# Compressing the cached pages with 512 columns in place of 256

## The chip, the cores and the metric

The kernel runs on one core of a Trainium2 chip. The metric is the device time of one execution in microseconds. Before the change it is 2870.46 us, the median of three runs (2867.37 to 2870.47).

## What is computed

The program is one step of a decoder layer: a half-step feed-forward network (SwiGLU), a mixer of RWKV-7 and sparse attention (NSA) in parallel, and a second feed-forward half-step, for 256 prompt tokens and 8 x 4 sampled ones, 288 columns in all. The change concerns the compression of the cached keys and values of the sampled sequences. Of the reference this is:

```python
blocks = kv_all[:, :, :2].reshape(b, n_cmp, CMP_BLOCK, 2, G, hd) + cmp_pe[:, :, None, :]
flat = blocks.transpose(0, 1, 3, 4, 2, 5).reshape(b, n_cmp, 2, G, CMP_BLOCK * hd)
hid = jax.nn.gelu(jnp.einsum('bnkgf,kfc->bnkgc', flat, cmp_w1))
kc = jnp.einsum('bnkgc,kcd->bnkgd', hid, cmp_w2)
```

A block is 32 positions of 128 features. There are 8 sequences with 8 pages of 128 positions, so 64 pages with 4 blocks and 2 heads each, which is 512 columns for the keys (k = 0) and 512 for the values (k = 1). Each column is the product of a 32 x 128 long vector with cmp_w1, which has 256 outputs, then GELU, then a product with cmp_w2.

## The kernel before

Every large product runs in split form: a float32 operand becomes a high part (rounded to the type fp32r) and a low part (the rest), and a product is the sum of three matmuls, high x high, low x high and high x low. Weights come in granules of 512 KB, four tiles of 128 x 256. `granule` (L71 to L82) loads one into `raw` (three slots) from the SP queue (L74), and for each half of it ScalarE casts the high part `whi` (L78) and VectorE subtracts to get the low part `wlo` (L80); each of these has four slots of half a granule. `dense_multi` (L129 to L148) takes a block of 256 outputs: two accumulators, and for each granule 24 matmuls with the weights stationary and 288 columns moving (L145 to L147). After each granule it calls `tick`.

Other work is woven into the dense products through a queue of generators. `tick` adds `K.rate` to a credit and takes a step of the first generator for each whole credit (L101 to L106). During the first feed-forward network, after its first pair of blocks, the queue holds `compress_cache`, with a rate of 0.7 (L1635); 256 ticks are left then. The order on each engine is set at compile time by a scheduler that works from this program order, and each engine takes its instructions in that order.

`compress_cache` goes through k = 0 and 1 and, for each, through two halves s of 32 pages. The pages of a half fill `craw`, a tile with one slot, in 8 steps of 4 pages; `page_loads` (L1026 to L1039) reads the page numbers into SP's registers (L1031) and issues one load of 128 KB for each page (L1039). Then come 32 steps, one for each position l of a block. In each ScalarE writes `cxh` (position embedding added, rounded, L1066), VectorE writes `cxl` (L1067), both 128 x 256 with three slots, and TensorE does six matmuls with 256 columns (L1072 to L1075), three for each half of the outputs, all into one bank `sc`. The weights cmp_w1 come through `granule`, a new one every four steps, 8 for each half. At the end of a half there are the GELU (L1080, L1090), the second product in full precision (L1083, L1098), a copy and a store.

Of the kernel before, what the change touches and what calls it, by code (L numbers as in the profile page):

```python
# [108 lines left out]
def drain(K, left=0):  # L109
    while len(K.queue) > left and step(K):  # L110
        pass
# [780 lines left out]
def pst(K, name):  # L892
    return K.ps.tile([128, 512], F32, name=name, bufs=2 if name == "sc" else 1)
# [133 lines left out]
def page_loads(K, pt, dst, src, p0, hist, lag=6, pool=False):  # L1027
    tc, nc = K.tc, K.nc
    n = dst.shape[1]
    eng, kind = (nc.gpsimd, mybir.EngineType.Pool) if pool else (nc.sync, mybir.EngineType.SP)  # L1030
    ins, vals = nc.values_load_multi_w_load_instructions(pt[0:1, p0:p0 + n], engines=[kind], min_val=0,  # L1031
                                                         max_val=src.shape[0] - 1)
    for q in ins:
        if not pool:
            follow(K, q, K.last_dma)
        if len(hist) >= lag:
            follow(K, q, hist[-lag])
    for i in range(n):
        hist.append(eng.dma_start(dst[:, i], src[bass.ds(vals[i], 1)].rearrange("a p f -> (a p) f")))  # L1039


def compress_cache(K, M, sp):
    tc, nc, a = K.tc, K.nc, K.a
    pt = sp.tile([1, 64], I32, name="pt0")
    follow(K, nc.sync.dma_start(pt, a["page_table"]), K.last_dma)
    ppe = sp.tile([128, 2, 32], F32, name="pe0")
    follow(K, nc.sync.dma_start(ppe, a["cmp_pe"]), K.last_dma)
    cw2 = sp.tile([128, 2, 2, 128], F32, name="cw20")
    follow(K, nc.sync.dma_start(cw2, a["cmp_w2"]), K.last_dma)
    hist = []  # L1050
    v8 = lambda t: t.rearrange("p (a b) -> p a b", b=8)
    for k in range(2):
        for s in range(2):
            raw = sp.tile([128, 32, 256], F32, name="craw", bufs=1)
            for p0 in range(0, 32, 4):
                page_loads(K, pt, raw[:, p0:p0 + 4], a["cache_cmp"][:, k], 32 * s + p0, hist)
                yield
            rv = raw.rearrange("p a (l g b) -> p a l (g b)", l=32, g=2)
            acc = pst(K, "sc")
            for gi in range(8):  # L1060
                for q, hi, lo in granule(K, a["cmp_w1"][k, gi]):
                    l = gi * 4 + q
                    pe = ppe[:, k, l:l + 1]
                    xh = sp.tile([128, 256], F32R, name="cxh", bufs=3)
                    xl = sp.tile([128, 256], F32R, name="cxl", bufs=3)
                    nc.scalar.activation(v8(xh), rv[:, :, l], AF.Identity, bias=pe)  # L1066
                    nc.vector.scalar_tensor_tensor(v8(xl), rv[:, :, l], pe, v8(xh.bitcast(F32)), op0=OP.add,  # L1067
                                                   op1=OP.subtract)
# [9 lines left out]
            hid = sp.tile([128, 2, 256], F32, name="chid", bufs=1)  # L1078
            if k == 0:
                nc.scalar.activation(hid.rearrange("p m c -> p (m c)"), acc, AF.Gelu_apprx_tanh)  # L1080
                pk = pst(K, "tp")[:, :256]
                for m in range(2):
                    nc.tensor.matmul(pk, cw2[:, 0, m], hid[:, m], start=m == 0, stop=m == 1)  # L1083
                kc = sp.tile([128, 256], F32, name="kc", bufs=1)
                nc.vector.tensor_copy(kc, pk)
                nc.gpsimd.dma_start(M.kcd[:, 256 * s:256 * s + 256], kc)
            else:
                for m in range(2):
                    for g in range(2):
                        nc.scalar.activation(  # L1090
                            hid[:, m].rearrange("p (b g a k) -> p b g a k", b=4, g=2, a=8)[:, :, g],
                            acc[:, 256 * m:256 * m + 256].rearrange("p (b a g k) -> p b a g k", b=4, a=8, g=2)[:, :, :, g],
                            AF.Gelu_apprx_tanh)
                for pk4 in range(2):
                    pk = pst(K, "tp")[:, :128]
                    for u in range(4):
                        for m in range(2):
                            nc.tensor.matmul(pk[32 * u:32 * u + 32], hid[:, m, 128 * pk4 + 32 * u:128 * pk4 + 32 * u + 32],  # L1098
                                             cw2[:, 1, m], start=m == 0, stop=m == 1, tile_position=(0, 32 * u))
                    vc = sp.tile([128, 128], F32, name="kc", bufs=1)  # L1100
                    nc.vector.tensor_copy(vc, pk)
                    nc.gpsimd.dma_start(M.vcd[:, 2 * s + pk4], vc)
            yield


def attn_prompt(K, M, pool):
# [506 lines left out]
def body(tc, a, o):  # L1613
    nc = tc.nc
    with ExitStack() as ctx:
        K = setup(tc, ctx, a)
        M = Ctx()
# [28 lines left out]
        with pool("x2") as xp:  # L1646
# [124 lines left out]
```

## Time and profile before

| | |
|---|---|
| median of the runs | 2870.46 us (2867.37 to 2870.47) |
| span of the profiled execution, first to last instruction | 2869.0 us |
| TensorE busy | 2800.4 us, 98% |
| VectorE busy | 1721.0 us, 60% |
| ScalarE busy | 1367.9 us, 48% |
| moved by DMA | 506.49 MB, mean 177 GB/s |
| first and last matmul line of the compression (L1072) | 84.2 and 867.8 us |

The profile gives no other time of the profiled execution than its span; it lies 1.5 us under the median of the runs, which were separate executions. Engine names in the rows: PE is TensorE's matmul, PEld its weight load, DVE VectorE, ACT ScalarE, POOL GpSimd, SPq the queue of SyncE that issues loads. A row of a timeline begins with the start in us and the time that it covers; "x3" means that three instructions are merged, and square brackets hold the idle time of the engine before it and what ended it. Matmul records overlap, since their durations are latencies.

### The profile page before, as it was taken

To read this page: it belongs to the slowest core of one execution; us is meant where nothing else is said; L and a number is where in the kernel's file an instruction comes from. 1 tells how busy PE (TensorE), PEld (TensorE's weight loads), DVE (VectorE), ACT (ScalarE), POOL (GpSimd) and SP (SyncE) were. 2 spreads that over 40 slices of the span, in tenths; PEclk is the share of its full clock that TensorE was granted. 3 is DMA by queue.
4 is the path that set the end of the run, shared out by engine and by line. 5 is a ranking of instruction groups with operands and counts; after the bars stand their busy time and mean duration, and the time that the engine had idled before them with its cause. 6 is when DMAs were issued, how large, how long until landed. Compare 5 with 4: busy or idle time off the path is not lost.

```text
span 2869.0 us, 57650 instructions
## 1 busy us (share of the span) xinstructions
PE 2800.4 (98%) x22257; PEld 2691.6 (94%) x22257; DVE 1721.0 (60%) x2950; ACT 1367.9 (48%) x2607; POOL 498.9 (17%) x686
## 2 busy tenths in 40 slices
PE   8999999999999899999999999998999999999997
PEld 8999999999999788998988978998999999999997
DVE  5565565655665777793585765655655455555555
ACT  5555555544555564532344644445444444434443
POOL 2000000000001456521133214112100000000002
PEclk9999999999999999998999999998999999999998
DMA  7557556557555443465446558563556555555553
GB/s 241 175 167 225 169 169 223 171 167 224 168 164 170 161 131 114 130 217 165 119 144 209 167 190 304 184 220 116 176 177 205 165 181 179 188 165 167 165 166 122
DMA packets 171751, 506.49 MB, mean 177 GB/s; under 512 B 28380, under 2 KB 55540, under 8 KB 171220
## 3 DMA queue, kind: packets, MB, share of 16 engines
q1 hardware_dynamic: 158516, 457.65, 50.4%
q0 software_dynamic: 12528, 44.27, 4.8%
q8 instruction: 174, 2.85, 0.4%
q14 instruction: 101, 0.83, 0.1%
q10 hardware_dynamic: 432, 0.88, 0.1%
HBM read 487.39 MB, written 23.66 MB: 178 GB/s over the span
## 4 chain that ended last, share of the span: by engine, by line
PE 93%; DVE 3%; DMA 1%; issue 1%; ACT 1%; POOL 0%; SPq 0%; DVEq 0%; POOLq 0%; ACTq 0%
PE acc L147 27%; PE acc L146 27%; PE acc L145 27%; PE sc L1075 1%; PE sc L1074 1%; PE sc L1072 1%; PE pv L1391 1%; DVE x L246 1%; DMA raw<-in_w_in_dram 1%; PE sc L656 1%; PE sc L1280 1%; DVE f L243 1%; DVE wlo L80 0%; DVE xlo L159 0%; PE sc L661 0%
## 5 line engine op out<-in xcount | busy, mean ns | idle before, releaser
L80 DVE TENSOR_TENSOR wlo<-raw,whi 128x512 fp32r<-128x512 f32 x1568 | 1111.5, 712 | 926.6 <-ACT whi L78 903.9
L78 ACT CAST whi<-raw 128x512 fp32r<-128x512 f32 x1568 | 964.2, 618 | 1202.4 <-PE acc L146 1077.4
L146 PE MATMUL acc<-xlo,whi 128*128 128x288 f32 x4208 | 1256.5, 299 | 12.1 <-DVE xlo L159 12.1
L145 PE MATMUL acc<-xhi,whi 128*128 128x288 f32 x4208 | 1251.3, 299 | 15.1 <-ACT whi L78 11.9
L147 PE MATMUL acc<-xhi,wlo 128*128 128x288 f32 x4208 | 1244.7, 300 | 10.3 <-DVE wlo L80 10.2
L145 PEld LDWEIGHTS acc<-xhi,whi 128*128 128x128 f32 x4208 | 797.7, 190 | 28.0 <-ACT whi L78 12.8
L146 PEld LDWEIGHTS acc<-xlo,whi 128*128 128x128 f32 x4208 | 798.3, 190 | 25.2 <-DVE xlo L159 13.7
L147 PEld LDWEIGHTS acc<-xhi,wlo 128*128 128x128 f32 x4208 | 792.1, 190 | 25.9 <-DVE wlo L80 13.0
L146 PE MATMUL acc<-hlo,whi 128*128 128x288 f32 x1408 | 416.1, 296 | 0.0
L145 PE MATMUL acc<-hhi,whi 128*128 128x288 f32 x1408 | 414.5, 295 | 0.0
L147 PE MATMUL acc<-hhi,wlo 128*128 128x288 f32 x1408 | 413.5, 296 | 0.0
L313 POOL TENSOR_TENSOR ut<-ut,rstd 128x288 f32<-128x288 f32 x88 | 79.7, 925 | 1364.6 <-ACT ut L312 1364.5
L145 PEld LDWEIGHTS acc<-hhi,whi 128*128 128x128 f32 x1408 | 265.0, 188 | 0.2 <-issue 0.2
L146 PEld LDWEIGHTS acc<-hlo,whi 128*128 128x128 f32 x1408 | 264.4, 188 | 0.2 <-issue 0.2
L147 PEld LDWEIGHTS acc<-hhi,wlo 128*128 128x128 f32 x1408 | 263.3, 188 | 0.0
L184 POOL TENSOR_TENSOR ssacc<-ssacc,sq 128x288 f32<-128x288 f32 x78 | 74.9, 960 | 240.3 <-ACT sq L180 237.5
L1067 DVE SCALAR_TENSOR_TENSOR cxl<-craw,pe,cxh 128x256 fp32r<-128x256 f32 x128 | 63.7, 502 | 47.9 <-ACT cxh L1066 41.4
L1066 ACT ACTIVATE cxh<-craw,pe 128x256 fp32r<-128x256 f32 x128 | 64.0, 506 | 53.8 <-PE sc L1075 44.1
L145 PE MATMUL acc<-ghi,whi 128*128 128x288 f32 x256 | 75.5, 295 | 0.0
L147 PE MATMUL acc<-ghi,wlo 128*128 128x288 f32 x256 | 75.3, 295 | 0.0
L146 PE MATMUL acc<-glo,whi 128*128 128x288 f32 x256 | 75.2, 294 | 0.0
L1075 PE MATMUL sc<-cxh,wlo 128*128 128x256 f32 x256 | 72.0, 281 | 0.0
(430 smaller groups left out, 2484.3 us busy)
## 6 DMA issues: line engine op xcount, KB each, us to landing
raw<-in_f_w_dram SPq DMA_DIRECT2D x528, 512.0 KB, 3.5
raw<-in_w_in_dram SPq DMA_DIRECT2D x156, 512.0 KB, 3.6
craw<-in_cache_cmp_dram SPq DMA_DIRECT2D x128, 128.0 KB, 3.8
raw<-in_cmp_w_dram SPq DMA_DIRECT2D x32, 512.0 KB, 4.4
raw<-in_w_out_dram SPq DMA_DIRECT2D x32, 512.0 KB, 3.6
craw<-in_cmp_w_dram POOLq DMA_DIRECT2D x16, 512.0 KB, 4.8
raw<-in_w_br_rw_dram SPq DMA_DIRECT2D x16, 512.0 KB, 5.3
vsel<-in_cache_sel_dram POOLq DMA_DIRECT2D x64, 128.0 KB, 3.9
```

The lines of the kernel that those rows point to most:

```text
L78: nc.scalar.copy(hi, r)
L80: nc.vector.tensor_sub(lo, r, hi.bitcast(F32))
L145: nc.tensor.matmul(ac[m], hi[:, ms], xhi[:, kt], start=first, stop=False)
L146: nc.tensor.matmul(ac[m], hi[:, ms], xlo[:, kt], start=False, stop=False)
L147: nc.tensor.matmul(ac[m], lo[:, ms], xhi[:, kt], start=False, stop=last)
L184: nc.gpsimd.tensor_tensor(self.acc, self.acc, sq, op=OP.add)
L243: return eng.tensor_tensor(u[:, s], u[:, s], r[:, None, :].to_broadcast([128, s.stop - s.start, NT]), op=OP.mult)
L246: return eng.tensor_tensor(x[:, s], x[:, s], u[:, s], op=OP.add)
L313: nc.gpsimd.tensor_tensor(t, t, rstd, op=OP.mult)
L1066: nc.scalar.activation(v8(xh), rv[:, :, l], AF.Identity, bias=pe)
L1067: nc.vector.scalar_tensor_tensor(v8(xl), rv[:, :, l], pe, v8(xh.bitcast(F32)), op0=OP.add, op1=OP.subtract)
L1075: nc.tensor.matmul(ac, lo[:, ms], xh, start=False, stop=l == 31, skip_group_check=True)
```

## The change

The two halves of the pages are no longer two halves of the columns but two halves of the positions: `half` 0 loads positions 0 to 15 of the blocks of all 64 pages, `half` 1 positions 16 to 31. A matmul then has 512 columns, and its two output halves get a bank each, both slots of `sc`. The weights of a position pass once for each k, so `granule` is called 16 times for cmp_w1 and no longer 32 times. A page load now takes half a page's rows: 64 KB, 128 rows of 512 bytes; there are 64 for each half, in 8 steps of 8. The number of steps falls from 160 to 96, and the rate is set to 0.42.

```diff
     for k in range(2):
-        for s in range(2):
-            raw = sp.tile([128, 32, 256], F32, name="craw", bufs=1)
-            for p0 in range(0, 32, 4):
-                page_loads(K, pt, raw[:, p0:p0 + 4], a["cache_cmp"][:, k], 32 * s + p0, hist)
+        accs = [pst(K, "sc") for _ in range(2)]
+        for half in range(2):
+            raw = sp.tile([128, 64, 128], F32, name="craw", bufs=1)
+            src = a["cache_cmp"][:, k, :, 128 * half:128 * half + 128]
+            for p0 in range(0, 64, 8):
+                page_loads(K, pt, raw[:, p0:p0 + 8], src, p0, hist)
                 yield
-            acc = pst(K, "sc")
-            for gi in range(8):
+            for gi in range(4 * half, 4 * half + 4):
                 for q, hi, lo in granule(K, a["cmp_w1"][k, gi]):
...
-                    xh = sp.tile([128, 256], F32R, name="cxh", bufs=3)
-                    xl = sp.tile([128, 256], F32R, name="cxl", bufs=3)
+                    xh = sp.tile([128, 512], F32R, name="cxh", bufs=3)
+                    xl = sp.tile([128, 512], F32R, name="cxl", bufs=3)
...
-                        ac = acc[:, 256 * m:256 * m + 256]
-                        nc.tensor.matmul(ac, hi[:, ms], xh, start=l == 0 and m == 0, stop=False,
-                                         skip_group_check=True)
-                        nc.tensor.matmul(ac, hi[:, ms], xl, start=False, stop=False, skip_group_check=True)
-                        nc.tensor.matmul(ac, lo[:, ms], xh, start=False, stop=l == 31, skip_group_check=True)
+                        nc.tensor.matmul(accs[m], hi[:, ms], xh, start=l == 0, stop=False)
+                        nc.tensor.matmul(accs[m], hi[:, ms], xl, start=False, stop=False)
+                        nc.tensor.matmul(accs[m], lo[:, ms], xh, start=False, stop=l == 31)
...
-            K.rate = 0.7
+            K.rate = 0.42
```

The GELU, the second product, the copy and the store are done once for each k on 512 columns, no longer once for each of two halves on 256.

Three places in the order of instructions, before and after. The first is TensorE at the first step of the compression (`sc` is the accumulator, `cxh` and `cxl` the pieces of activations, `whi` and `wlo` the weights, `acc` the dense product). Before:

```order
L1072 MATMUL sc_1311<-cxh_1318,whi_1314 128x256
L145 MATMUL acc_1276<-xhi_73,whi_1330 128x288
L1074 MATMUL sc_1311<-cxl_1319,whi_1314 128x256
L146 MATMUL acc_1276<-xlo_74,whi_1330 128x288
L147 MATMUL acc_1275<-xhi_73,wlo_1332 128x288
L1075 MATMUL sc_1311<-cxh_1318,wlo_1316 128x256
```

And with the change:

```order
L1072 MATMUL sc_612<-cxh_1965,whi_1961 128x512
L145 MATMUL acc_1890<-xhi_73,whi_1977 128x288
L1073 MATMUL sc_612<-cxl_1966,whi_1961 128x512
L146 MATMUL acc_1890<-xlo_74,whi_1977 128x288
L147 MATMUL acc_1889<-xhi_73,wlo_1979 128x288
L1074 MATMUL sc_612<-cxh_1965,wlo_1963 128x512
```

The pattern is the same with half the matmuls at twice the columns; the other three of the step go into sc_613.

The second place is the SP queue at the end of the page loads of the second filling of `craw`, from the weight load after which the last pages come (`raw` from in_f1_w2 is a weight of the feed-forward network, in_cmp_w1 the compression's own; ISA rows are register instructions). Before:

```order
L74 DMA raw_4000<-in_f1_w2_dram 128x1024
L1039 ISA
L1039 DMA craw_3394<-in_cache_cmp_dram 128x256
L1031 TENSOR_LOAD pt0_572
L1031 ISA x8
L1039 ISA
L1039 DMA craw_3394<-in_cache_cmp_dram 128x256
L74 DMA raw_4075<-in_f1_w2_dram 128x1024
```

Three more pages follow, and then the weight loads go on. With the change:

```order
L74 DMA raw_4788<-in_f1_w2_dram 128x1024
L1031 ISA x10
L1039 ISA
L1039 DMA craw_3541<-in_cache_cmp_dram 128x128
L1039 ISA
L1039 DMA craw_3541<-in_cache_cmp_dram 128x128
L1039 ISA
L1039 DMA craw_3541<-in_cache_cmp_dram 128x128
L74 DMA raw_4822<-in_f1_w2_dram 128x1024
```

Five more pages follow here: eight pages lie behind the weight load raw_4788, where five lay behind raw_4000. At the first filling eight pages and 12 register instructions lie there, at the third eight and 8, each in place of five pages, a register load and 8 register instructions; at the fourth eight pages, a register load and 16 register instructions, in place of seven pages, a register load and 8.

The third place is ScalarE at the start of the same half, where the first activations of the new `craw` are written. Before:

```order
L78 CAST whi_3923<-raw_3921 128x512
L78 CAST whi_3939<-raw_3921 128x512
L78 CAST whi_4002<-raw_4000 128x512
L1066 ACTIVATE cxh_4150<-craw_3394,pe0_574 128x256
L1066 ACTIVATE cxh_4194<-craw_3394,pe0_574 128x256
L1066 ACTIVATE cxh_4246<-craw_3394,pe0_574 128x256
L78 CAST whi_4018<-raw_4000 128x512
```

And with the change:

```order
L78 CAST whi_4675<-raw_4673 128x512
L78 CAST whi_4691<-raw_4673 128x512
L78 CAST whi_4790<-raw_4788 128x512
L1067 ACTIVATE cxh_4862<-craw_3541,pe0_608 128x512
L1067 ACTIVATE cxh_4944<-craw_3541,pe0_608 128x512
L1067 ACTIVATE cxh_5060<-craw_3541,pe0_608 128x512
L338 COPY f_481<-acc_4450 128x288
```

In both, three pieces of activations stand between the two casts of one granule's halves; the second cast, whi_4806 from raw_4788, comes behind the copy. VectorE has its three pieces in the same place, between the two subtractions. At the first and third fillings it is the same; at the fourth both halves of the granule are cast ahead of the three pieces with the change, and one half before.

## Rows read from the trace of the kernel before

**Rows 1.** The page: busy us, share of the span and instructions of each engine.

```profile
PE 2800.4 (98%) x22257; PEld 2691.6 (94%) x22257; DVE 1721.0 (60%) x2950; ACT 1367.9 (48%) x2607; POOL 498.9 (17%) x686
```

**Rows 2.** Busy time by windows (us), with counts, granted clock, DMA share, GB/s.

```profile
36.00:100.00 64.00, 64.00 (x487) 64.00 (x486) 36.82 (x65) 33.05 (x61) 5.59 (x6) 1.00 0.74 227
...
900.00:940.00 40.00, 40.00 (x302) 40.00 (x301) 20.91 (x33) 21.66 (x43) 7.88 (x10) 1.00 0.53 163
```

**Rows 3.** Timeline of TensorE, dense and compression matmuls.

```profile
86.00 0.29 PE L145 MATMUL acc<-xhi,whi 128*128 128x288 f32 x1
...
89.59 0.28 PE L1072 MATMUL sc<-cxh,whi 128*128 128x256 f32 x1
...
95.69 0.28 PE L1072 MATMUL sc<-cxh,whi 128*128 128x256 f32 x1
...
96.04 0.30 PE L145 MATMUL acc<-xhi,whi 128*128 128x288 f32 x1
```

**Rows 4.** Timeline of TensorE, the second product of the compression.

```profile
254.46 1.02 PE L1083 MATMUL tp<-chid,cw 128*128 128x256 f32 x4
```

**Rows 5.** Groups of instructions from 36 to 860 us: busy us, mean ns.

```profile
L80 DVE TENSOR_TENSOR wlo<-raw,whi 128x512 fp32r<-128x512 f32 x521 | 364.1, 702 | 290.3 <-ACT whi L78 284.0 <-PE sc L194 0.9
L78 ACT CAST whi<-raw 128x512 fp32r<-128x512 f32 x520 | 320.6, 620 | 340.3 <-PE acc L146 279.0 <-DMA raw<-in_f_w_dram 28.3 <-PE sc L1074 22.6
...
L1066 ACT ACTIVATE cxh<-craw,pe 128x256 fp32r<-128x256 f32 x128 | 64.0, 506 | 53.8 <-PE sc L1075 44.1 <-DMA craw<-in_cache_cmp_dram 4.4 <-DMA raw<-in_f_w_dram 2.7
L1067 DVE SCALAR_TENSOR_TENSOR cxl<-craw,pe,cxh 128x256 fp32r<-128x256 f32 x128 | 63.7, 502 | 47.9 <-ACT cxh L1066 41.4 <-DMA raw<-in_f_w_dram 4.0 <-DMA raw<-in_cmp_w_dram 2.5
```

**Rows 6.** Timeline of the SP queue in the second page phase.

```profile
270.54 1.37 SPq L1039 DMA_DIRECT2D craw<-in_cache_cmp_dram  x3
272.01 0.38 SPq L74 DMA_DIRECT2D raw<-in_f_w_dram  x1
272.58 2.24 SPq L1039 DMA_DIRECT2D craw<-in_cache_cmp_dram  x2
...
275.55 1.96 SPq L1039 DMA_DIRECT2D craw<-in_cache_cmp_dram  x3
```

**Rows 7.** Timeline of ScalarE at the start of the second half.

```profile
276.85 0.62 ACT L78 CAST whi<-raw 128x512 fp32r<-128x512 f32 x1 [0.98 <-PE acc L146]
278.45 0.62 ACT L78 CAST whi<-raw 128x512 fp32r<-128x512 f32 x1 [0.98 <-PE acc L146]
281.13 1.31 ACT L1066 ACTIVATE cxh<-craw,pe 128x256 fp32r<-128x256 f32 x3 [2.06 <-DMA craw<-in_cache_cmp_dram]
282.35 1.13 ACT L78 CAST whi<-raw 128x512 fp32r<-128x512 f32 x2
```

**Rows 8.** Timeline of VectorE at the same place.

```profile
281.67 1.28 DVE L1067 SCALAR_TENSOR_TENSOR cxl<-craw,pe,cxh 128x256 fp32r<-128x256 f32 x3 [1.88 <-DMA raw<-in_f_w_dram]
282.99 1.29 DVE L80 TENSOR_TENSOR wlo<-raw,whi 128x512 fp32r<-128x512 f32 x2
```

**Rows 9.** ScalarE's last cast ahead of the first, third and fourth half.

```profile
73.06 0.62 ACT L78 CAST whi<-raw 128x512 fp32r<-128x512 f32 x1 [0.96 <-PE acc L146]
...
484.27 0.62 ACT L78 CAST whi<-raw 128x512 fp32r<-128x512 f32 x1 [1.07 <-PE acc L147]
...
690.43 0.62 ACT L78 CAST whi<-raw 128x512 fp32r<-128x512 f32 x1 [0.98 <-PE acc L146]
```

**Rows 10.** VectorE's first subtraction behind the pieces of the same three halves.

```profile
78.20 2.53 DVE L80 TENSOR_TENSOR wlo<-raw,whi 128x512 fp32r<-128x512 f32 x4
...
489.74 0.68 DVE L80 TENSOR_TENSOR wlo<-raw,whi 128x512 fp32r<-128x512 f32 x1
...
695.22 1.90 DVE L80 TENSOR_TENSOR wlo<-raw,whi 128x512 fp32r<-128x512 f32 x3
```

**Rows 11.** DMA issues: KB each, median us from issue to landing.

```profile
kcd<-kc POOLq DMA_DIRECT2D x2, 128.0 KB, 3.8
vcd<-kc POOLq DMA_DIRECT2D x4, 64.0 KB, 3.2
```

More of the change, by code (lines that the diff above doesn't have):

```diff
@@ L1052, in compress_cache @@
     for k in range(2):
-        for s in range(2):
-            raw = sp.tile([128, 32, 256], F32, name="craw", bufs=1)
-            for p0 in range(0, 32, 4):
-                page_loads(K, pt, raw[:, p0:p0 + 4], a["cache_cmp"][:, k], 32 * s + p0, hist)
+        accs = [pst(K, "sc") for _ in range(2)]
[4 more added lines that the diff above has]
+                page_loads(K, pt, raw[:, p0:p0 + 8], src, p0, hist)
                 yield
-            rv = raw.rearrange("p a (l g b) -> p a l (g b)", l=32, g=2)
-            acc = pst(K, "sc")
-            for gi in range(8):
+            rv = raw.rearrange("p a (l b) -> p a l b", b=8)
+            for gi in range(4 * half, 4 * half + 4):
                 for q, hi, lo in granule(K, a["cmp_w1"][k, gi]):
@@ L1063, in compress_cache @@
                     pe = ppe[:, k, l:l + 1]
-                    xh = sp.tile([128, 256], F32R, name="cxh", bufs=3)
-                    xl = sp.tile([128, 256], F32R, name="cxl", bufs=3)
-                    nc.scalar.activation(v8(xh), rv[:, :, l], AF.Identity, bias=pe)
-                    nc.vector.scalar_tensor_tensor(v8(xl), rv[:, :, l], pe, v8(xh.bitcast(F32)), op0=OP.add,
+                    xh = sp.tile([128, 512], F32R, name="cxh", bufs=3)
+                    xl = sp.tile([128, 512], F32R, name="cxl", bufs=3)
+                    nc.scalar.activation(v8(xh), rv[:, :, l % 16], AF.Identity, bias=pe)
+                    nc.vector.scalar_tensor_tensor(v8(xl), rv[:, :, l % 16], pe, v8(xh.bitcast(F32)), op0=OP.add,
                                                    op1=OP.subtract)
@@ L1076, in compress_cache @@
+                        nc.tensor.matmul(accs[m], hi[:, ms], xl, start=False, stop=False)
+                        nc.tensor.matmul(accs[m], lo[:, ms], xh, start=False, stop=l == 31)
                     if l < 31:
                         yield
[L1078 to L1102, printed above, removed]
@@ L1103, in compress_cache @@
-            yield
+        hid = sp.tile([128, 2, 512], F32, name="chid", bufs=1)
+        if k == 0:
+            for m in range(2):
+                nc.scalar.activation(hid[:, m], accs[m], AF.Gelu_apprx_tanh)
+            pk = pst(K, "tp")
+            for m in range(2):
+                nc.tensor.matmul(pk, cw2[:, 0, m], hid[:, m], start=m == 0, stop=m == 1)
+            kc = sp.tile([128, 512], F32, name="kc", bufs=1)
+            nc.vector.tensor_copy(kc, pk)
+            nc.gpsimd.dma_start(M.kcd, kc)
+        else:
+            for m in range(2):
+                for g in range(2):
+                    nc.scalar.activation(hid[:, m].rearrange("p (b g a k) -> p b g a k", b=8, g=2, a=8)[:, :, g],
+                                         accs[m].rearrange("p (b a g k) -> p b a g k", b=8, a=8, g=2)[:, :, :, g],
+                                         AF.Gelu_apprx_tanh)
+            vc = sp.tile([128, 512], F32, name="kc", bufs=1)
+            pk = pst(K, "tp")
+            for b in range(4):
+                for u in range(4):
+                    for m in range(2):
+                        nc.tensor.matmul(pk[32 * u:32 * u + 32, 128 * b:128 * b + 128],
+                                         hid[:, m, 128 * b + 32 * u:128 * b + 32 * u + 32], cw2[:, 1, m],
+                                         start=m == 0, stop=m == 1, tile_position=(0, 32 * u))
+            nc.vector.tensor_copy(vc, pk)
+            nc.gpsimd.dma_start(M.vcd, vc.rearrange("p (b f) -> p b f", b=4))
@@ L1106, in attn_prompt @@
+        yield
 def attn_prompt(K, M, pool):
```

## The prediction

> **What bounds the kernel now.** I read the page first: TensorE is busy 98% of the span, VectorE 60% and ScalarE 48% [rows 1]. A share over the whole run says little, so next I cut out the stretch in which the changed work runs. From 36 us, when the first pages are asked for, to 860 us TensorE has no idle time in any window, and the clock is 1.00; the first of these windows stands in [rows 2], with a later one without any compression. So in this stretch time is worth only what it is worth on TensorE: either a matmul gets cheaper there, or something else gets so late that TensorE has to wait.
>
> Then the spacing of matmuls, start to start, in the timeline. Between 86.00 and 89.59 us, 27 matmuls with 288 columns start: 3.59/27 = 0.133 us each; the window from 900 to 940 us gives 40/302 = 0.1325 [rows 2, 3]. Three with 256 columns, one behind the other, take 95.69 to 96.04: 0.117 us each [rows 3]. I use 132.8 and 118 ns. The durations on the page (some 300 ns) are latencies and overlap; they are no cost.
>
> **The change, part by part.**
>
> *TensorE.* 768 matmuls with 256 columns become 384 with 512. The columns stay 196,608; what may go is a cost per matmul. The trace has no matmul of this form with 512 columns, so I bound it. A line through the two spacings has a slope of (132.8 - 118)/32 = 0.46 ns a column and no constant left over: 118 + 256 x 0.46 = 236 ns, gain 384 x (2 x 118 - 236) = 0. Lower end: four matmuls of the second layer, in full precision with 256 columns, take 1.02 us with 0.378 us for the last one: (1.02 - 0.378)/3 = 0.214 us each, 512 cycles at 2.4 GHz and no surplus [rows 4]. If 512 columns here run as densely, the gain is 384 x (236 - 214) = 8.4 us. I see no reason for a loss. The two spacings of the same form are nearer to the question than a row of another form; with their reading errors I take 234 ns, **a gain of 0.8 us**. The Trainium skill (TensorE: Matmul & The Clock Gate, section Back-to-back issue gap) gives a warm gap of columns/2.4 plus 2.5 ns, which would be 109 ns for 256 columns and 216 for 512. The rows do not agree at 256, so I do not use it; it stands among the rivals by its mechanism, a cost per matmul that long streams hide.
>
> *Splits of weights.* 32 granules become 16: 32 casts of 618 to 620 ns on ScalarE and 32 subtractions of 702 to 712 on VectorE go [rows 5], 20 and 23 us, and 8 MB of loads. The pieces of activations halve in number, 128 to 64 each, at double width: between 1x and 2x the 0.506 and 0.502 us of one [rows 5]. All of it is work beside a TensorE that never waits: **worth nothing**, as long as TensorE stays covered. The second-layer matmuls keep their columns; fewer copies and stores are off the path. The steps go from 160 to 96 and the rate from 0.7 to 0.42, so both queues last 229 of the 256 ticks.
>
> *Page loads on SP.* 128 become 256, at half the bytes and with rows of 512 bytes. One page costs SP (1.37 - 0.33)/2 = 0.52 us; the register part of a step of four costs 2.24 - 0.33 - 0.52 = 1.39 us [rows 6]. A step is thus 3.5 us, at 0.7 steps a tick; with eight pages 8 x 0.52 + about 2.4 = 6.6 us, at 0.42. With one weight load of about 0.4 us [rows 6], SP needs 2.8 us of a tick before and 3.2 after. A tick without compression matmuls is 24 x 0.1328 = 3.19 us. **SP goes from nine tenths of TensorE's pace to all of it** in the four page phases. Behind a page load on SP stand the weight loads.
>
> *The start of each half.* Here I expect the cost. ScalarE takes its work in order. At 281.13 us it begins the first three pieces of activations, after 2.06 us of waiting for the last page; the next weights' cast stands behind them and starts at 282.35 [rows 7]. VectorE does its three pieces from 281.67 and the subtraction for these weights, 0.69 us, only from 282.99 to 283.68 [rows 8]. When does TensorE want it? A half granule is used up every 1.60 us (276.85 to 278.45), and the cast of 278.45, released by TensorE, took the slot just freed, the fourth. The next slot was free at 280.05, so its weights are wanted at 280.05 + 3 x 1.60 = 284.85, the low part two matmuls later, at 285.1. **1.4 us are to spare.** The same sum at the other three starts [rows 9, 10], the low part being due 1.60 + 4.80 + 0.27 = 6.67 us after the last cast: due 79.73, done 78.89, spare 0.8; due 490.94, done 490.42, spare 0.5; due 697.10, done 695.91, spare 1.2.
>
> After the change three things move there. First, the order of SP: between the weight load whose half is cast last and the last page there were 5 pages, 8 register instructions with their load, and a weight load; now 8 pages, 12, 10 and 8 register instructions and a weight load at the first three starts. With 0.52 a page and an estimate of 0.13 per register instruction that is 1.7, 1.5 and 1.2 us later. At the fourth it is 1.5 later, but both halves are cast ahead, worth 1.6. Second, a load of 64 KB lands sooner than one of 128: 3.2 against 3.8 us for stores of this stage [rows 11], so 0.6 back. Third, three pieces of 512 columns: VectorE spaces three of 256 by (1.28 - 0.50)/2 = 0.4 us, so I take 0.8 for 512 (the lower end is a plain subtraction at that width, 0.7 [rows 5]); with the first ScalarE piece longer by 0.3 to 0.4 this is 1.5 us more. TensorE then waits 1.7 - 0.6 + 1.5 - 0.8 = 1.8, 1.5 - 0.6 + 1.5 - 1.4 = 1.0, 1.2 - 0.6 + 1.5 - 0.5 = 1.6 and 0 us: **4.4 us in all**. Lower end: 0, if ScalarE is further ahead there than now. Upper end: without the 0.6 back it is 6.2 us, and a lagging SP adds to that.
>
> **Sum.** The profiled span is 2869.0 us, 1.5 under the median of the runs, 2870.5, and within their spread. 2869.0 - 0.8 + 4.4 = 2872.6; carried to the median, **2874.1 us**, slower by 0.13%. About 0.2% (5.7 us) is what a measurement of this kernel tells from no change. Behind this stretch the instruction order of the mixer shifts by a few rows; I put nothing on it, and 2 us either way into the range.
>
> **The rivals.**
>
> *Everything stays covered.* The casts saved let ScalarE and VectorE run further ahead, and the spare times suffice. Only the 0.8 us remain: 2869.7. For it: TensorE does not wait once now, and fewer bytes move per tick. Against: the slots for split weights are four as before, so nobody can run further ahead than now.
>
> *A cost per matmul goes away.* TensorE gets 384 x 20 to 22 us nearer the lower end: minus 4 (about 225 ns per matmul, a constant of 11 to 12 ns over 2.4 GHz each) to minus 8.4. With the waits covered 2862.1 to 2866.5; with them 2866.5 to 2871. For it: the full-precision rows run without a surplus. Against: the surplus over 2.4 GHz is larger at 288 columns (12.8 ns) than at 256 (11.3), as a rate would have it.
>
> *SP becomes the supply.* If page loads take SP more than the 0.52 us, weights come slower than TensorE uses them, all through a page phase of some 60 us. It decides from about 0.05 us more per page: 64 x 0.05 = 3.2 us a phase is what whole prefetch slots can carry. Three pages took 1.96 in place of 1.37 us once in the trace [rows 6]; at that rate in each group of six pages a phase loses 6 us, of which some 3 are carried; with the 4.4 that is 2870.5 - 0.8 + 4.4 + 4 x 1.5 to 4 x 3, 2880 to 2886.
>
> **How the numbers follow.** My forecast, waits of 2 to 7 us, 0.48: 2871.7 to 2876.7. Everything covered 0.26; a cost per matmul gone 0.14; SP the supply 0.12. The range leaves out most of the last and the end of the third: 2864.5 to 2880. Slower by over 0.2% (above 2876.2): nearly all of SP's 0.12 and about a fifth of the forecast's 0.48, 0.21. Faster by over 0.2% (below 2864.7): half of the third and little else, 0.08. Within: 0.71.
>
> **What would show it.** Right: compression matmuls 0.23 to 0.24 us apart; idle time of TensorE of 1 to 2 us shortly behind the last page of a half, with the low weights on VectorE as releaser, and ScalarE held there for 3 us by a page load. Wrong: spacing of 0.214 to 0.225; no wait of TensorE before 860 us; or waits spread all over the page phases with weight loads late on SP.

## The result, and the profile after

The changed kernel takes **2890.89 us** (median of 4 runs, 2887.52 to 2893.74) against 2870.47 for the kernel before (4 runs, 2867.37 to 2871.09): a ratio of 1.0069 with a 95% interval of 1.0057 to 1.0081. That is slower by 20 us, beyond the upper end of the range, 2880. The profiled execution has a span of 2887.9 us, 18.9 more than before.

The page first: busy TensorE, the clock by slices, and the chain.

```profile
PE 2806.4 (97%) x21869; PEld 2676.1 (93%) x21869; DVE 1686.3 (58%) x2850; ACT 1327.9 (46%) x2503; POOL 493.7 (17%) x682
...
PEclk9999999999999899998999999998999999999998
...
PE 89%; DVE 4%; SPq 2%; DMA 2%; issue 1%; ACT 1%; POOL 0%; ACTq 0%; DVEq 0%
```

Against [rows 1], VectorE and ScalarE have less work, as the change says. What is new is SyncE's queue in the chain of work that ended last, with 2%. The windows of the changed kernel say where it went (columns as in [rows 2]: length, then busy us and instructions of TensorE, its weight loads, VectorE, ScalarE and GpSimd, granted clock, DMA share, GB/s).

```profile
36.00:860.00 824.00, 813.10 (x5802) 793.56 (x5802) 431.65 (x684) 374.59 (x650) 39.43 (x43) 0.99 0.55 175
109.00:119.00 10.00, 7.88 (x46) 7.12 (x44) 6.28 (x10) 5.61 (x11) 1.86 (x2) 0.83 0.41 146
318.00:328.00 10.00, 6.66 (x32) 6.43 (x31) 5.30 (x8) 5.54 (x11) 0.00 (x0) 0.66 0.47 154
529.00:535.00 6.00, 2.90 (x20) 2.43 (x19) 3.54 (x6) 4.02 (x7) 0.00 (x0) 1.00 0.29 103
739.00:747.00 8.00, 5.66 (x29) 5.19 (x29) 6.55 (x12) 5.43 (x10) 0.00 (x0) 0.80 0.57 194
```

Between 36 and 860 us TensorE had no idle time before; now it has 824.00 - 813.10 = 10.9 us, and it lies in the four short windows, one for each half, shortly behind its last page. In three of the four the clock falls as well. Here is the second of them, in TensorE's timeline.

```profile
318.30 0.29 PE L147 MATMUL acc<-hhi,wlo 128*128 128x288 f32 x1
321.93 0.61 PE L145 MATMUL acc<-hhi,whi 128*128 128x288 f32 x1 [3.34 <-ACT whi L78]
322.33 0.44 PE L146 MATMUL acc<-hlo,whi 128*128 128x288 f32 x1
...
327.13 0.38 PE L145 MATMUL acc<-hhi,whi 128*128 128x288 f32 x1
327.35 0.30 PE L146 MATMUL acc<-hlo,whi 128*128 128x288 f32 x1
```

TensorE waits 3.34 us for a cast on ScalarE. Then its matmuls start 0.24 us apart, 1.2 GHz for 288 columns, up to 327.13, where they go back to 0.13. So one wait costs twice: the idle time, and 2.2 us of slow clock. SyncE's queue ahead of that wait:

```profile
307.31 2.17 SPq L74 DMA_DIRECT2D raw<-in_f_w_dram  x2
310.94 1.41 SPq L1039 DMA_DIRECT2D craw<-in_cache_cmp_dram  x3
312.45 1.25 SPq L74 DMA_DIRECT2D raw<-in_f_w_dram  x1
313.90 2.81 SPq L1039 DMA_DIRECT2D craw<-in_cache_cmp_dram  x5
```

ScalarE's timeline:

```profile
311.24 1.14 ACT L78 CAST whi<-raw 128x512 fp32r<-128x512 f32 x2 [2.91 <-DMA raw<-in_f_w_dram]
315.45 0.62 ACT L78 CAST whi<-raw 128x512 fp32r<-128x512 f32 x1 [3.07 <-PE acc L147]
319.13 1.94 ACT L1067 ACTIVATE cxh<-craw,pe 128x512 fp32r<-128x512 f32 x3 [3.06 <-DMA craw<-in_cache_cmp_dram]
...
321.26 0.61 ACT L78 CAST whi<-raw 128x512 fp32r<-128x512 f32 x1
```

And VectorE's:

```profile
319.89 2.08 DVE L1068 SCALAR_TENSOR_TENSOR cxl<-craw,pe,cxh 128x512 fp32r<-128x512 f32 x3 [3.08 <-ACT cxh L1067]
321.91 2.71 DVE L80 TENSOR_TENSOR wlo<-raw,whi 128x512 fp32r<-128x512 f32 x4
```

ScalarE stands 3.06 us before the page that SyncE asked for last, then does three pieces in 1.94 us; the cast that TensorE needs stands behind them and starts at 321.26. In the kernel before, the wait at this start was 2.06 us and TensorE did not notice [rows 7]. The difference shows ahead of it: at 311.24 ScalarE had just waited 2.91 us for weights, and at 315.45 again 3.07. The profile puts this second wait down to a matmul, but the weights that are cast there were asked for at 309.15 and landed at 315.36 by the trace, and TensorE ran out of weights 3 us behind this cast: it too was a wait for weights, and not for TensorE to free a slot. Over 36 to 960 us, ScalarE's waits for transfers in the changed kernel (us in total, times, longest):

```profile
ACT whi L78 <- DMA raw<-in_f_w_dram: 92.0, 57, 3.6
ACT cxh L1067 <- DMA craw<-in_cache_cmp_dram: 16.4, 4, 5.2
```

Before, these were 28.3 us in 18 waits and 4.4 us in 2 [rows 5]. So weights come late off SyncE's queue, mostly in the page phases: some 52 of the 92 us lie there, in 30% of the stretch. Its timeline in the first of them:

```profile
77.57 0.95 SPq L1039 DMA_DIRECT2D craw<-in_cache_cmp_dram  x2
...
79.19 2.92 SPq L1039 DMA_DIRECT2D craw<-in_cache_cmp_dram  x6
82.20 1.65 SPq L74 DMA_DIRECT2D raw<-in_f_w_dram  x2
85.83 0.87 SPq L1039 DMA_DIRECT2D craw<-in_cache_cmp_dram  x2
...
94.02 4.84 SPq L1039 DMA_DIRECT2D craw<-in_cache_cmp_dram  x8
...
102.59 0.87 SPq L1039 DMA_DIRECT2D craw<-in_cache_cmp_dram  x2
```

From one step of eight pages to the next it takes 8.26, 8.19 and 8.57 us. TensorE gives a step 3.19/0.42 = 7.6 us. Over the four whole phases, from first to last page, SyncE takes 62.0, 65.1, 66.1 and 67.9 us and issues 75 weight loads in them: 3.48 us for each, where TensorE uses one in 3.19. In the kernel before it was 136.3 us for 42, 3.25 each.

The register part of a step can be read by itself. These are the register instructions of the page numbers between 44 and 110 us (duration in ns: shortest, median, longest):

```profile
L1031 SPq FUSED_REGOPS  x58: 147/147/159, 44.0 to 102.2; - x58
L1031 SPq TENSOR_LOAD <-pt x7: 525/529/542, 50.1 to 99.4; - x7
```

Start to start, a load takes 0.58 us and each of the eight reads behind it, a FUSED_REGOPS and a short check, 0.255 us: 2.6 us for a step.

The matmuls themselves did what was forecast: the compression matmuls shown occupy 0.24 and 0.23 us to the next start, where one of 256 columns took 0.117 [rows 3].

```profile
331.08 0.40 PE L1073 MATMUL sc<-cxl,whi 128*128 128x512 f32 x1
331.32 0.29 PE L146 MATMUL acc<-hlo,whi 128*128 128x288 f32 x1
331.45 0.40 PE L1074 MATMUL sc<-cxh,wlo 128*128 128x512 f32 x1
331.68 0.29 PE L147 MATMUL acc<-hhi,wlo 128*128 128x288 f32 x1
```

For a balance I added up, for every matmul until the first feed-forward layer ends, the time to the next start, by kind (us). Two of the experiments below stand beside the two kernels; some 1.3 us of other matmuls are the same in all.

| | before | after | pages on GpSimd | the same, four PSUM tiles |
|---|---|---|---|---|
| first matmul starts | 8.0 | 9.6 | 7.5 | 8.3 |
| feed-forward, 288 columns, 6336 | 851.6 | 871.6 | 854.4 | 852.5 |
| compression, 256 or 512 columns | 91.1 | 89.3 | 89.3 | 89.3 |
| second layer of the keys | 1.4 | 0.9 | 0.9 | 0.9 |
| second layer of the values | 2.4 | 4.8 | 4.8 | 2.7 |
| last matmul of the layer starts | 955.6 | 977.3 | 958.0 | 954.8 |

The layer ends 21.7 us later. 20.0 of it lie in the feed-forward matmuls: most of it waits and slow clock, and 1.8 beside the second layer of the values, whose last records stand singly between them (the last experiment shows these rows); 2.4 lie in that second layer itself; 1.5 in a later first matmul, which varies by as much between the other profiled executions; the wide matmuls and the keys give back 1.8 and 0.4. Of 21.7, 2.8 do not reach the end of the program; the time behind this layer differs by a few us from one profiled execution to the next.

"TensorE's excess" in the expectations is a sum of the same kind: the starts between 36 and 960 us, each less the usual spacing of its columns (133, 118 and 233 ns). It was 1.7 us before and 20.7 after. Where a single surplus is above 0.15 us I count it as a wait, else as slow clock: at the four starts that makes 3.0 + 3.8 + 3.4 + 2.7 = **12.8 us of waits** (more than the 10.9 us idle of the window, where a matmul's latency of 0.3 us counts as busy) **and 1.4 + 2.2 + 0.2 + 1.7 = 5.5 us of slow clock**.

### The profile page after: what moved, and what is told of

It reads as the page before. It is cut to its first block, busy times and chain, and to the rows that moved or that the text cites. A ratio compares the mean times of both kernels' runs of the same rounds, so it can differ in the third digit from the quotient of the medians.

```text
span 2887.9 us, 57227 instructions
## 1 busy us (share of the span) xinstructions
PE 2806.4 (97%) x21869; PEld 2676.1 (93%) x21869; DVE 1686.3 (58%) x2850; ACT 1327.9 (46%) x2503; POOL 493.7 (17%) x682
## 4 chain that ended last, share of the span: by engine, by line
PE 89%; DVE 4%; SPq 2%; DMA 2%; issue 1%; ACT 1%; POOL 0%; ACTq 0%; DVEq 0%
PE acc L147 26%; PE acc L145 26%; PE acc L146 26%; SPq L1039 1%; PE sc L1073 1%; PE sc L1074 1%; PE sc L1072 1%; PE pv L1391 1%; DVE wlo L80 1%; DVE x L246 1%; DMA raw<-in_f_w_dram 1%; SPq L1031 1%; DMA raw<-in_w_in_dram 1%; PE sc L656 1%; DVE xlo L159 1%
## 5 line engine op out<-in xcount | busy, mean ns | idle before, releaser
L80 DVE TENSOR_TENSOR wlo<-raw,whi 128x512 fp32r<-128x512 f32 (+1 forms) x1536 | 1093.9, 716 | 964.1 <-ACT whi L78 926.6
L78 ACT CAST whi<-raw 128x512 fp32r<-128x512 f32 (+1 forms) x1536 | 943.0, 618 | 1255.7 <-PE acc L146 1062.8
L146 PEld LDWEIGHTS acc<-xlo,whi 128*128 128x128 f32 x4208 | 798.9, 190 | 27.0 <-DVE xlo L159 13.5
L1068 DVE SCALAR_TENSOR_TENSOR cxl<-craw,pe,cxh 128x512 fp32r<-128x512 f32 x64 | 48.1, 762 | 63.0 <-ACT cxh L1067 59.0
L1067 ACT ACTIVATE cxh<-craw,pe 128x512 fp32r<-128x512 f32 x64 | 45.4, 720 | 60.9 <-PE sc L1074 44.4
L1073 PE MATMUL sc<-cxl,whi 128*128 128x512 f32 x128 | 50.6, 395 | 0.0
```

The costliest lines, as they stand in the source:

```text
L78: nc.scalar.copy(hi, r)
L80: nc.vector.tensor_sub(lo, r, hi.bitcast(F32))
L146: nc.tensor.matmul(ac[m], hi[:, ms], xlo[:, kt], start=False, stop=False)
L1067: nc.scalar.activation(v8(xh), rv[:, :, l % 16], AF.Identity, bias=pe)
L1068: nc.vector.scalar_tensor_tensor(v8(xl), rv[:, :, l % 16], pe, v8(xh.bitcast(F32)), op0=OP.add, op1=OP.subtract)
L1073: nc.tensor.matmul(accs[m], hi[:, ms], xl, start=False, stop=False)
```

## The experiments

Five of the kernels below (fixed page numbers, the kernel before with the changed kernel's page traffic, the two empty steps, the two rates) were executed once, in the profiled execution; for them the span stands, and the excess says more than the span, since spans of the kernel before lay between 2863 and 2874 us beside them. The others have 8 to 11 runs, and ratios are to runs of the kernel before beside them.

The theory after the result: SyncE needs more time to issue a step's pages than TensorE gives it, so weights and pages come late, ScalarE has nothing in hand when it comes to the last page of a half, and waits there in its order. The rivals: the in-order wait and the wider pieces do it whatever SyncE does; or the short rows of 512 bytes are slow to land.

**Pages at fixed numbers, one transfer a step.** This kernel leaves out the lookup of the page numbers.

```diff
-                page_loads(K, pt, raw[:, p0:p0 + 8], src, p0, hist)
+                hist.append(nc.sync.dma_start(raw[:, p0:p0 + 8], src[p0:p0 + 8].rearrange("a p f -> p a f")))
+                follow(K, hist[-1], K.last_dma)
```

> The changed kernel, but the eight pages of a step are loaded by one transfer at fixed page numbers: the same bytes in the same rows of 512, 32 issues on SyncE in place of 256, and no register instruction for them. It leaves out the lookup of the page table. If SyncE's time for issuing pages is what makes the last page and the weights late, TensorE's excess between 36 and 960 us (20.7 us in the changed kernel, waits and slow clock together) falls below 3, and the span is 2865 to 2871. If short rows or the memory traffic make the pages late, or the wider pieces hold ScalarE and VectorE, the excess stays at 10 or more and the span at 2878 or more.

Measured: span 2869.3 us, excess 2.3. The window of this kernel, columns as above:

```profile
36.00:860.00 824.00, 824.00 (x5913) 806.12 (x5913) 445.96 (x701) 382.59 (x664) 39.95 (x43) 1.00 0.57 178
```

TensorE does not wait once, with the same bytes in the same short rows and the same wide pieces. The rows and the pieces alone cost nothing; the 256 issues with their register instructions do (which of the two was not separated). Late landing is not the reason either: in the page phases a weight load landed 4.0 us (median) after its issue in the changed kernel, 4.9 in the kernel before and 4.0 in the kernel with pages on GpSimd below, which does not wait.

**Four pages to a step.**

```diff
-            for p0 in range(0, 64, 8):
-                page_loads(K, pt, raw[:, p0:p0 + 8], src, p0, hist)
+            for p0 in range(0, 64, 4):
+                page_loads(K, pt, raw[:, p0:p0 + 4], src, p0, hist)
...
-            K.rate = 0.42
+            K.rate = 0.56
```

> The changed kernel with four pages to a step, so 16 page steps in a half, and a rate of 0.56 in place of 0.42, so that the queue lasts as many ticks. Pages, issues and bytes are the same, but a tick of a page phase holds 0.56 x (1.39 + 4 x 0.52) + 0.4 = 2.3 us of SyncE's time in place of 3.2. If SyncE's lag in the page phases is the cause, its queue is no longer behind when the last page is asked for; then only the forecast's in-order wait with the wider pieces is left, 0 to 4.4 us: 2868 to 2875. If the in-order wait is enough by itself for the whole cost, whatever SyncE has behind it, the time stays at 2885 to 2893.

Measured: 2870.12 us, ratio to the kernel before 1.0002 (0.9992 to 1.0011). TensorE is busy for all of 36 to 860 us. ScalarE's waits of this kernel over 36 to 960 us:

```profile
ACT whi L78 <- DMA raw<-in_f_w_dram: 17.9, 11, 2.3
ACT cxh L1067 <- DMA craw<-in_cache_cmp_dram: 5.3, 4, 2.0
```

All 256 issues are still there, over a longer time, and the cost is gone. ScalarE still stands up to 2.0 us before a last page with three wide pieces behind it, and that does not reach TensorE: without SyncE's lag the forecast's own 4.4 us are 0.

**The kernel before, with the changed kernel's page traffic.**

```diff
-            for p0 in range(0, 32, 4):
-                page_loads(K, pt, raw[:, p0:p0 + 4], a["cache_cmp"][:, k], 32 * s + p0, hist)
+            for p0 in range(0, 32, 2):
+                page_loads(K, pt, raw[:, p0:p0 + 2], a["cache_cmp"][:, k], 32 * s + p0, hist, halves=True)
...
+            for h in (0, 128):
+                hist.append(eng.dma_start(dst[:, i, h:h + 128],
+                                          src[:, :, h:h + 128][bass.ds(vals[i], 1)].rearrange("a p f -> (a p) f")))
...
-            K.rate = 0.7
+            K.rate = 0.84
```

> The kernel before, with 256 columns moving and its weights split twice, but each page is loaded as two transfers with rows of 512 bytes, two pages to a step, and the rate is 0.84 so that a page phase lasts 19 ticks as in the changed kernel: 256 issues at the changed kernel's pace, 3.1 us of SyncE in a tick of 3.19. If the number of issues on SyncE is the cause, TensorE waits at the four starts as in the changed kernel, and the span grows by 8 to 20 us, to 2877 to 2889. If the three wider pieces behind the last page are the cause, the excess of TensorE stays within 3 us and the span at 2868 to 2873.

Measured: span 2877.9 us, 8.9 more than before, excess 12.7. Its waits, ScalarE's over 36 to 960 us and TensorE's over 36 to 860:

```profile
ACT cxh L1071 <- DMA craw<-in_cache_cmp_dram: 13.8, 4, 4.8
PE acc L145 <- ACT whi L78: 4.6, 4, 2.2
PE acc L147 <- DVE wlo L80: 1.2, 3, 0.8
```

The narrow matmuls with the weights split twice become slow in the same way, at three of the four starts: the page loads do it without the rest of the change. It is the lower end of what was expected, about half the cost of the changed kernel by the span and somewhat more by the excess (11.0 of 19.0 us above the kernel before); whether the other half is due to the wider pieces on top of a late SyncE or to the steps being smaller was not separated.

**Two empty steps behind the last page.**

```diff
+            for _ in range(2):
+                yield
             rv = raw.rearrange("p a (l b) -> p a l b", b=8)
```

> The changed kernel with two empty steps between the last page of a half and its first piece of activations: 104 steps at the same rate of 0.42, some 4.8 ticks or 15 us in which ScalarE and VectorE meet no page. SyncE's page phases are as dense as before. If the cost comes only where ScalarE waits in order for the last page, the waits at the four starts go, TensorE's excess falls from 20.7 to under 4 us, and the span is 2866 to 2872. If SyncE is so late in the page phases that the weight loads themselves starve TensorE, TensorE waits as much without the in-order wait: an excess of 12 or more and a span of 2880 or more.

Measured: span 2875.1 us, excess 12.5, between the two expectations; and the edit did not do what it was for. The compression's instructions have priority, and the first piece kept its place in ScalarE's order at the first start, directly behind the same cast as in the changed kernel. SyncE's last page there is issued at 104.43, and ScalarE's row is:

```profile
107.54 1.95 ACT L1069 ACTIVATE cxh<-craw,pe 128x512 fp32r<-128x512 f32 x3 [4.02 <-DMA craw<-in_cache_cmp_dram]
```

What it did move is the compression's weight load, five loads back on SyncE. So it says nothing for or against the in-order wait, which the next kernel takes away. But ScalarE still stood 13.5 us in all before pages here, SyncE's phases were little shorter (61.5 to 64.4 us), and 8 us of the excess went: the place of that weight load, directly behind the last page in the changed kernel, may be part of the price. One execution does not settle how much.

**The first piece behind the cast of its own weights.**

```diff
-        nc.scalar.copy(hi, r)
+        K.last_cast = nc.scalar.copy(hi, r)
...
-                    nc.scalar.activation(v8(xh), rv[:, :, l % 16], AF.Identity, bias=pe)
+                    act = nc.scalar.activation(v8(xh), rv[:, :, l % 16], AF.Identity, bias=pe)
+                    if l % 16 == 0:
+                        follow(K, act, K.last_cast)
```

> The changed kernel with one order more: the first piece of activations of a half comes on ScalarE behind the cast of its own weights, in place of directly behind the last page, which puts some five casts of the running weights ahead of it. SyncE's stream stays as it is, with its lag. If a late SyncE costs time only through ScalarE standing before the last page, the waits at the four starts go: an excess of 2 to 6 us and a time of 2868 to 2875. If the weights are simply late behind SyncE's page loads, the excess stays at 14 or more and the time at 2882 to 2893.

Measured: 2875.22 us, 0.2 us beyond the range expected, ratio 1.0018 (1.0009 to 1.0028); profiled span 2868.4, excess 4.2. The profiled execution is the fastest of ten (2870.34 to 2880.48 us), so its rows show the better side of this kernel. ScalarE's timeline at the second start:

```profile
313.97 0.62 ACT L78 CAST whi<-raw 128x512 fp32r<-128x512 f32 x1 [2.75 <-DMA raw<-in_cmp_w_dram]
314.49 1.95 ACT L1067 ACTIVATE cxh<-craw,pe 128x512 fp32r<-128x512 f32 x3
316.35 1.64 ACT L78 CAST whi<-raw 128x512 fp32r<-128x512 f32 x3
```

Its waits for weights over 36 to 960 us:

```profile
ACT whi L78 <- DMA raw<-in_f_w_dram: 92.1, 62, 3.2
```

SyncE is as late as in the changed kernel (92.1 us of waits against 92.0), yet TensorE idles only 0.6 us in 36 to 860. So at this lag both are needed: a SyncE that is late, and ScalarE standing before the page with the running weights behind it. Either taken away, most of the 20 us go: here 16 by the medians, and where the 4 that stay lie was not placed.

**Page loads on GpSimd.**

```diff
-                page_loads(K, pt, raw[:, p0:p0 + 8], src, p0, hist)
+                page_loads(K, pt, raw[:, p0:p0 + 8], src, p0, hist, pool=True)
```

> The changed kernel with the 256 page loads and their register instructions issued by GpSimd in place of SyncE; SyncE issues weight loads alone. Bytes, rows, rate and pieces stay. If SyncE's issue time is the cause, TensorE's excess between 36 and 960 us falls from 20.7 to the 2.3 us of the kernels without a wait (the second layers' matmuls), and the time is 2867 to 2873. If GpSimd is as slow at issuing pages, the last page of a half is late there too and ScalarE waits in order for it: some 10 us stay, 2877 to 2885.

Measured: 2868.29 us, ratio 0.9991 (0.9981 to 1.0000), excess 2.5; TensorE is busy for all of 36 to 860 us and ScalarE never waits for a page. GpSimd had only 39.4 us of work in that stretch of the changed kernel. (`pool` also drops the order of the page numbers behind the last weight load, which is on another queue now.)

**The pace of the pages.** Two kernels change only the rate.

```diff
-            K.rate = 0.42
+            K.rate = 0.39
```

> The changed kernel with a rate of 0.39 in place of 0.42. In the changed kernel's first page phase SyncE took 8.34 us from one step of eight pages to the next (77.57 to 102.59 us, three steps) where 1/0.42 ticks of 3.19 us give 7.6: a lag of 0.7 us a step. At 0.39 a step has 8.2 us of TensorE's time, so the lag falls to 0.2 or less a step. If the lag is the cause, the excess falls from 20.7 to under 8 us, span 2867 to 2876. If not, it stays within 4 us of the changed kernel's, span 2884 or more.

Measured: span 2878.7 us, excess 14.9: less than the changed kernel, but the forecast of under 8 us failed. The first page phase took 62.0 us from first to last page at 0.39 as at 0.42 (43.5 to 105.5, and 44.7 to 106.7): SyncE still set its own pace there and gained no lead, and ScalarE still stood 5.4 us before one page. That little more time is not enough.

```diff
-            K.rate = 0.42
+            K.rate = 0.5
```

> The changed kernel with a rate of 0.50 in place of 0.42: a step of eight pages has 6.4 us of TensorE's time and needs some 7.9 us of SyncE's, a lag of 1.5 us a step in place of 0.5 to 0.7, 12 us a phase in place of 4 to 6. If the lag is the cause, TensorE waits 6 to 8 us more in each of the four phases, spread over them, and the span grows by 20 to 35 us over the changed kernel's 2887.9. If only the order behind the last page costs, the span stays within 5 us of it.

Measured: span 2886.2 us, excess 21.0, so the cost hardly grew, and that expectation failed. (The changed kernel's 20.7 hold 1.8 beside the second layer of the values, which this kernel does not have; without them the growth is some 2 us.) TensorE's waits over 36 to 860 us:

```profile
PE acc L145 <- ACT whi L78: 8.5, 8, 2.4
PE sc L1072 <- ACT whi L78: 3.0, 2, 1.8
PE acc L147 <- DVE wlo L80: 1.0, 5, 0.2
```

The waits for ScalarE are ten and spread over the phases, as a starved supply makes them, while ScalarE's longest wait for a page fell to 2.4 us. SyncE took 8.1 us a step again (first pages of seven steps from 48.71 to 97.43), so its lag by the sum is 1.7 us a step, 14 a phase, and TensorE lost some 5 a phase. The loaded and split weights in hand are the likely place of the rest; that was not measured. A lag this large costs without a long stand. Together with the kernel of the order above this speaks for two ways to lose: a large lag uses up what is in hand, and a small one is made dear by the stand before the last page.

**Can it beat both?** First the kernel before with the same cure.

```diff
-                page_loads(K, pt, raw[:, p0:p0 + 4], a["cache_cmp"][:, k], 32 * s + p0, hist)
+                page_loads(K, pt, raw[:, p0:p0 + 4], a["cache_cmp"][:, k], 32 * s + p0, hist, pool=True)
```

> The kernel before with its 128 page loads issued by GpSimd in place of SyncE: 256 columns moving, weights split twice. It gives what the wide matmuls are worth once the queue is out of the way. TensorE never waited in the kernel before, so moving its page loads alone should change nothing: 2867 to 2874, the same within 0.2%. If SyncE's queue cost the kernel before something that its TensorE does not show, it is faster by 5 us or more.

Measured: 2874.49 us, ratio 1.0018 (1.0009 to 1.0027): no gain, rather 4 us lost, and half a us beyond the range expected. TensorE is idle for 0.1 us of 36 to 860, and the first layer ends at 956.6; where the 4 us lie stays open.

Then the changed kernel with pages on GpSimd and the second layer of the values in four tiles.

```diff
-                page_loads(K, pt, raw[:, p0:p0 + 8], src, p0, hist)
+                page_loads(K, pt, raw[:, p0:p0 + 8], src, p0, hist, pool=True)
...
-            pk = pst(K, "tp")
             for b in range(4):
+                pk = pst(K, "tp")[:, :128]
                 for u in range(4):
                     for m in range(2):
-                        nc.tensor.matmul(pk[32 * u:32 * u + 32, 128 * b:128 * b + 128],
+                        nc.tensor.matmul(pk[32 * u:32 * u + 32],
...
-            nc.vector.tensor_copy(vc, pk)
+                nc.vector.tensor_copy(vc[:, 128 * b:128 * b + 128], pk)
```

> The changed kernel with its page loads on GpSimd, and the second layer of the values in four PSUM tiles of 128 columns with four copies, in place of one tile of 512 with one copy. In the kernel with one tile its last 20 of 64 records ran in pairs between matmuls of the first layer, 0.41 us a pair, and the 64 together took 4.8 us where the kernel before took 2.4. With four tiles they stand in groups of eight, and 2 us of TensorE's excess around 870 us go. The time is 2863 to 2871, 0 to 0.2% under the kernel before; if the pairs cost nothing, 2866 to 2873.

Measured: **2864.88 us, ratio 0.9979 (0.9969 to 0.9990)**, faster than both kernels. TensorE's timeline with one tile (the kernel with pages on GpSimd):

```profile
869.02 1.54 PE L1098 MATMUL tp<-cw,chid 128*32 128x128 f32 x44
870.49 0.40 PE L145 MATMUL acc<-xhi,whi 128*128 128x288 f32 x1
870.82 0.41 PE L1098 MATMUL tp<-cw,chid 128*32 128x128 f32 x2
871.15 0.40 PE L146 MATMUL acc<-xlo,whi 128*128 128x288 f32 x1
871.48 0.41 PE L1098 MATMUL tp<-cw,chid 128*32 128x128 f32 x2
```

And with four tiles, where other rows lie between the two:

```profile
869.10 0.66 PE L1098 MATMUL tp<-cw,chid 128*32 128x128 f32 x14
...
873.20 0.66 PE L1098 MATMUL tp<-cw,chid 128*32 128x128 f32 x16
```

A pair between two matmuls of the first layer makes the three starts cover 0.66 us, where 16 records in a row take as much. The table shows the 2.1 us that come back in the second layer and 1.9 in the feed-forward matmuls, nearly all of them beside the pairs, and the wide matmuls' 1.8 that then remain. The layer ends only 0.8 us earlier than in the kernel before, though, and the medians differ by 5.3 (2.9 to 8.9 by the interval); what of that lies behind this layer was not placed.

## Why the prediction was wrong

*TensorE.* Right, and a little small: 234 ns a matmul was forecast, 232.6 came, a gain of 91.1 - 89.3 = 1.8 us against 0.8. The rival in which a cost per matmul goes away is out. The Trainium skill's warm gap (TensorE: Matmul & The Clock Gate, section Back-to-back issue gap), which it calls the gap of an isolated matmul, makes 216 ns of 512 columns: the rows do not agree with it there either.

*Splits of weights: worth nothing.* The balance bears it out: in the kernels without a wait the layer's end moves by no more than the matmuls and the second layer give.

*Page loads on SP.* **This is the step that failed**: "SP goes from nine tenths of TensorE's pace to all of it", 3.2 us a tick. It came to 3.48 us a tick, more than TensorE's 3.19, and the sum held nothing for a SyncE that is late. The single prices were low by little. A page does cost 0.52 us (six in a row in 2.92). The register part is 2.6 us in place of 2.4. A weight load takes 0.48 with what stands beside it (0.67 us from the page issue that ends at 78.52 to the one at 79.19, less the 0.19 that lie between two pages anyway) in place of 0.4. That alone is 8 x 0.52 + 2.6 + 2.38 x 0.48 = 7.9 us a step, 3.3 a tick, where the forecast had 6.6 + 2.38 x 0.4 = 7.6. The rest are single issues, one to four in each phase, that took 0.9 to 1.5 us in place of some 0.35 (the eight pages at 94.02 took 4.84 us, 0.9 more than their price, all of it before the second), and waits of SyncE for a free slot. A small miss, but at a queue that is full it decides. The text even gave the point: 0.05 us more a page makes SyncE the supply, and 0.7 us a step is 0.09 a page. This rival got 0.12; it should have been the likeliest, since the forecast itself put the queue at its limit with nothing in reserve. It did not come as written either: it had TensorE wait all through the page phases and 2880 to 2886 us, and the waits came at the four starts.

*The start of each half.* The place was right (idle time of TensorE shortly behind the last page, ScalarE held 3 us by a page), the releaser mostly not: it was the high weights' cast, and VectorE's subtraction only twice, for 0.4 us in all. The size was wrong on both sides. The forecast took ScalarE's lead from the kernel before and moved it by the few instructions in between: 4.4 us. With SyncE in time it is 0, as the kernels with fixed page numbers, with four pages a step and with GpSimd's queue show. With SyncE late it is 12.8 us. So the forecast had the place right with half of the cause, and that half alone costs nothing here. Two of its smaller terms were too dear: VectorE spaces three of the wide pieces by 0.67 us, not 0.8 (2.08 us in all at 319.89), and a page of half the size landed 0.9 us sooner, not 0.6 (median 2.9 us against 3.8).

*The clock.* Not in the sum at all: 5.5 us, since the matmuls behind a wait start 0.24 us apart for a while. No wait stood in [rows 2], so nothing in the trace before had to show it; but a sum that forecasts waits should have left room for it.

*Second layer: "keep their columns".* True, and yet 2.4 us dearer, with 1.8 more in the matmuls beside them, because of the order in which they stand between others. Bytes, columns and counts do not show that.

*Sum.* The whole miss is 2890.9 - 2874.1 = 16.8 us: waits 12.8 in place of 4.4, slow clock 5.5, the values' second layer 2.4 and the matmuls beside it 1.8, together 18.1, less 1.0 for the matmuls, 17.1. What is left over, and the start and the end of the program, which differ by a few us between executions, one pair of profiles cannot place.

## What to carry to other kernels

Where a change brings a queue to the pace of the engine that it feeds, treat the queue as the new bound: price each issue and each register instruction from rows, and ask what the reserve was used for. A small lag costs little by itself; look for the place where an engine that works in order must stand before the lagging queue's last transfer, with other work behind it. Before giving up such a change, move the issues to an idle queue or spread them: here the same matmuls with pages on GpSimd and the second layer in groups went from 20 us slower to 0.2% faster.

## What the runs showed of the hardware

A wait of TensorE of 1.8, 3.34 and 2.16 us (behind the first, second and last start) was followed by some 3 to 5 us at 1.2 GHz, 1.4 to 2.2 us of loss each (behind the first and the last the slow matmuls begin 0.4 and 1.8 us after the wait has ended); the one of 2.92 us at 530 was not (clock 1.00 in 529 to 535, and the row at 533.58 stands 0.13 behind its predecessor). The length of the wait alone does not decide it; what does, these runs do not show.

Two records of a second layer in full precision, 128 columns each, cost 0.66 us with the matmul beside them when they stand alone between the first layer's, and 16 of them in a row cost about as much.
